# Moving the PEER gate product to ScalarE and writing a sigmoid gate as a tanh

## The chip, the cores and the metric

The kernel runs on one core of one Trainium2 chip, in one launch. A core has TensorE (PE in the profile, with its weight loads as PEld), VectorE (DVE), ScalarE (ACT), GpSimd (POOL), SyncE (SP) and 16 DMA engines that move data between HBM and the on-chip memories. The metric is the device time of one execution in microseconds, as a median over runs. All arithmetic is float32 in and out.

## The reference, cut to what matters

The network is a first block (three attention branches, then a PEER feed-forward layer) and a second block of two layers (an mLSTM and a retention mixer, each followed by an expert-choice mixture of experts, for a context and a latent sequence). Everything has 256 tokens of width 1024. Two places matter here. In the PEER layer every token picks 128 of 16384 experts (8 heads, 16 each). An expert is one row of `u` and one row of `v`:

```
act = gelu(einsum('chkd,cd->chk', u[ic], hc), approximate=False)
w   = gc * act                                 # gc: softmax of the picked scores
out = einsum('chk,chkd->cd', w, v[ic])
```

In the mLSTM mixer the output of every head (128 wide) is divided by its root mean square and multiplied by a sigmoid gate `o`, a projection of the input:

```
y = y * rsqrt(mean(y*y, axis=-1) + EPS)        # per token and head, EPS = 1e-6
y = y * norm_g * sigmoid(o)
```

## The kernel before, in words

The kernel is written in a tile framework. A program's Python generators issue instructions, and the framework simulates each engine's time line to order them; every engine then runs its own list strictly in that order, waiting on semaphores where an operand is not there. So a change of one instruction's engine can reorder others.

**Picks.** The function `picks` works through two blocks of 128 tokens and, in each, 128 picks: pick k is the k-th expert of each of the 128 tokens, one token per partition. A pick is this chain:

1. POOL issues an indirect DMA (L1359) that gathers one row of 2048 numbers per partition, `u` and `v` side by side, 1 MB in all, into one of RING = 8 buffers.
2. DVE multiplies the `u` half by the token's input and sums it into one number per partition (the `stt` at L1360; by the helper's line, 128x1024 at L614 in the profile).
3. ACT takes the gelu of that 128x1 column (L1363; L598 in the profile).
4. DVE multiplies the column by the pick's gate (`tt`, L1364; L605 in the profile, 128x1).
5. ACT scales the 128x128 identity by the column (L1368), which gives a diagonal matrix. There are four such buffers.
6. PE multiplies the diagonal with the `v` half, two matmuls of 128x512 (L1370; L617 in the profile), and adds them up in PSUM over the 128 picks.

When step 6 has read the buffer, POOL may issue a gather into it. The first gather of a pick is thus released eight picks earlier by PE.

Beside the picks runs other work through `drive(..., [side], PACE)`: the routing of the heads (queries, top-16 searches on DVE, `prepare`, `prepare_last`, `route`), and the whole context side of the second block's first layer (`context_task`: an mLSTM with its projections, gates, convolution, attention by heads, the norm below, output projection and the opening of its mixture of experts). These use the same DVE, ACT, POOL and PE, and stand between the picks' instructions in each engine's list.

**Output gates.** `mlstm_norm` runs twice: for the context beside the picks, and for the latent sequence in the stage after them, beside `mlstm_attend`. Each run goes over two slabs of four heads, and each slab over two tiles of 128 tokens, so there are eight tiles of 128x512 in all. For every tile the projection stands in PSUM; ACT takes exp(-o), DVE adds one (L1890, by the helper L609) and takes a reciprocal (L1891). `norm_pair` then makes the root of the mean square for two heads and multiplies head, root and gate. The function is called for the retention layer too, with another gate.

In the profile, an operation that goes through a helper has the helper's line: `act` L598, `tt` L605, `ts` L609 and L611, `stt` L614, `mm` L617. ACT needs a function's table loaded before it can run it; a load (ACT_TABLE_LOAD) stands in ACT's list wherever the next function is not in the set that is there.

Of the kernel before, what the change touches and what calls it, by code (L numbers as in the profile page):

```python
# [14 lines left out]
AF = mybir.ActivationFunctionType  # L15
OP = mybir.AluOpType
AX = mybir.AxisListType

EPS = 1e-6
# [3 lines left out]
RING, BATCH = 8, 1  # L23
# [490 lines left out]
class K:  # L514
# [817 lines left out]
    def picks(self, h2, prep):  # L1332


        ident = self.c("ident")
        ring = dg = None
        for i, r in enumerate(self.routes):
            while r["heads"] < 1:
                yield next(prep) * 0
            if ring is None:  # L1340
                ring, dg = deque(self.f(2048, True) for _ in range(RING)), deque(self.f(128, True) for _ in range(4))
            if i:
                self.nc.sync.dma_start(h2[0].a, self.keep[2])
            po = self.ps(2)
            rows, gate, act = (r[n].a for n in ("rows", "gate", "act"))
            for k in range(0, 128, BATCH):
                while r["heads"] * 16 < k + 1:
                    yield next(prep) * 0
                if i and k == 128 - BATCH:

                    ring.popleft().free()
                    self.x = [self.f(1024) for _ in range(2)]
                    self.nc.sync.dma_start(self.x[0].a, self.keep[0])
                got = []
                for j in range(k, k + BATCH):
                    b = ring[0].a
                    ring.rotate(-1)
                    got.append(b)
                    self.nc.gpsimd.indirect_dma_start(b, None, self.t["puv"], bass.IndirectOffsetOnAxis(ap=rows.bitcast(U32)[:, j:j + 1], axis=0))  # L1359
                    self.stt(b[:, :1024], b[:, :1024], 1.0, h2[0].a, OP.mult, OP.mult, accum_out=act[:, j:j + 1])  # L1360
                    yield 2600
                o = act[:, k:k + BATCH]
                self.act(o, o, AF.Gelu)  # L1363
                self.tt(o, o, gate[:, k:k + BATCH], OP.mult)  # L1364
                for j, b in enumerate(got):
                    d = dg[0].a
                    dg.rotate(-1)
                    self.act(d, ident, AF.Copy, scale=act[:, k + j:k + j + 1])  # L1368
                    for f in range(2):
                        self.mm(po.a[:, f * 512:(f + 1) * 512], d, b[:, 1024 + f * 512:1024 + (f + 1) * 512], k + j == 0, k + j == 127)  # L1370
            if i == 0:
                x = ring[0].a[:, :1024]
                ring.rotate(-1)
            else:
                x = self.x[1].a
            self.nc.sync.dma_start(x, self.keep[i])
            for f in range(2):
                o = x[:, f * 512:(f + 1) * 512]
                self.tt(o, po.a[:, f * 512:(f + 1) * 512], o, OP.add)
            if i == 0:  # L1380
                self.nc.sync.dma_start(self.keep[0], x)
            po.free()
            for n in ("rows", "gate", "act"):
                r[n].free()
        h2[0].free()
        for b in (*ring, *dg):
            b.free()
# [492 lines left out]
    def mlstm_norm(self, S):  # L1880

        S["yT"] = self.r(2048), self.r(2048)
        for s in range(2):

            b = self.f(1024)
            for i, p in enumerate(self.wide([S["hT"]], self.halves("w2", 8 + 2 * s, S["seg"]))[0]):
                o = b.a[:, i * 512:(i + 1) * 512]
                self.act(o, p.a, AF.Exp, scale=-1.0)
                p.free()
                self.ts(o, o, 1.0, OP.add)  # L1890
                self.nc.vector.reciprocal(o, o)  # L1891
            if s == 1:
                for x in S["hT"]:
                    x.free()
            yield 9800
            for j in (4 * s, 4 * s + 2):
                while S.get("heads", 0) < j + 2:
                    yield 5200
                self.norm_pair(S["y"], b, 512, j % 4 * 128, S["ss"].a[:, :16].rearrange("p (i h) -> p i h", i=2)[:, :, j:j + 2], j)
                self.pair_T(S["yT"], [S["y"].a[:, i * 1024:(i + 1) * 1024] for i in range(2)], j, self.col("mlstm_g"))  # L1900
                yield 3000
            b.free()
        for b in (S["ss"], S["y"]):
            b.free()

    def norm_pair(self, y, gate, w, o, ss, j):

        t = self.f(16)
        v4 = t.v("p (k i h) -> p k i h", k=4, i=2)
        self.ts(v4[:, 0], ss, 1.0 / 128, OP.mult, EPS, OP.add)  # L1910
        out = t.a[:, 8:12]
        self.root(out, t.a[:, 4:8], t.a[:, :4])
        for i in range(2):
            for h in range(2):
                k = slice(i * 1024 + (j + h) * 128, i * 1024 + (j + h + 1) * 128)
                self.stt(y.a[:, k], y.a[:, k], out[:, 2 * i + h:2 * i + h + 1], gate.a[:, i * w + o + h * 128:i * w + o + h * 128 + 128], OP.mult, OP.mult)
        t.free()
# [553 lines left out]
```

## Time and profile before

| | us |
|---|---|
| median of 3 runs | 2615.86 (2615.13 to 2617.09) |
| profiled execution, its own time | 2619.42 |
| its span, first to last instruction | 2617.7 |
| PE busy | 2265.2 |
| DVE busy | 1243.2 |
| ACT busy | 802.9 |
| POOL busy | 634.4 |
| DMA, mean rate over the span | 328 GB/s |

The picks stage lies at about 411 to 1208 us of the span, the latent mLSTM stage at about 1208 to 1400, and the latent and retention layers behind it. Busy shares are averages over stages with different limits, so the stages have to be read by themselves. In a table of windows the granted clock (PEclk) is TensorE's clock as a share of 2.4 GHz (1.00 is 2.4, 0.50 is 1.2 GHz).

### The profile page before, as it was taken

The numbers are of one execution on the slowest core, as the hardware profiler recorded it, in microseconds if no ns is written. First come the engines' busy times: TensorE is split into PE (matmuls) and PEld (weight loads), VectorE is DVE, ScalarE is ACT, GpSimd is POOL, SyncE is SP. The second block draws the span as 40 slices with busy tenths as digits, with TensorE's granted clock in tenths as the row PEclk, the third lists the DMA queues.
The fourth block names the chain that finished last, engine by engine and source line by source line (L and its number), as shares of the span: only waits on it lengthen the run. The fifth ranks groups of instructions, "written<-read, shape, count | busy, mean of one in ns | idle before, by whom it ended". The sixth has DMA issues, their size and how long they took to land. (4 is left out here: it accounts for less than half of the span.)

```text
span 2617.7 us, 29085 instructions
## 1 busy us (share of the span) xinstructions
PE 2265.2 (87%) x10507; PEld 1276.5 (49%) x10507; DVE 1243.2 (47%) x2943; ACT 802.9 (31%) x1632; POOL 634.4 (24%) x526
## 2 busy tenths in 40 slices
PE   7999987799787789777878999999969989878877
PEld 5867776356332445224666344444459863222223
DVE  4365448899955676555866122212186461000001
ACT  5564443344622763223643000000042441000000
POOL 3223444344343444332530000000032420000000
PEclk9999988999999899999998999999989999999999
DMA  7467758898999789996446899999966398999997
GB/s 295 177 240 258 262 185 324 329 364 333 332 410 419 288 338 394 421 421 251 143 163 266 354 396 420 414 421 421 373 235 240 105 378 334 420 419 420 419 420 319
DMA packets 129534, 858.81 MB, mean 328 GB/s; under 512 B 15342, under 2 KB 15934, under 8 KB 33520
## 3 DMA queue, kind: packets, MB, share of 16 engines
q1 hardware_dynamic: 87120, 573.50, 55.2%
q0 software_dynamic: 42272, 283.47, 27.8%
q8 instruction: 83, 1.36, 0.2%
q14 instruction: 59, 0.48, 0.0%
HBM read 853.63 MB, written 3.28 MB: 327 GB/s over the span
## 5 line engine op out<-in xcount | busy, mean ns | idle before, releaser
L617 PE MATMUL pp<-fa 128*128 128x512 f32 (+10 forms) x4912 | 1289.2, 492 | 220.8 <-ACT fa L598 153.0
L617 PEld LDWEIGHTS pp<-fa 128*128 128x128 f32 (+3 forms) x4912 | 554.0, 159 | 836.5 <-issue 395.3
L617 PE MATMUL pp<-rw,rt 128*128 128x512 f32 (+1 forms) x1896 | 469.6, 401 | 17.4 <-ACT rw L598 5.6
L614 DVE SCALAR_TENSOR_TENSOR fa<-fa 128x1024 f32<-128x1024 f32 (+5 forms) x561 | 406.4, 747 | 109.0 <-DMA fa<-in_puv,fa 104.6
L605 POOL TENSOR_TENSOR rw<-fa,rw 128x1024 fp32r<-128x1024 f32 x84 | 211.5, 2519 | 809.4 <-ACT rw L598 772.0
L617 PEld LDWEIGHTS pp<-rw,rt 128*128 128x128 f32 x1896 | 351.1, 190 | 114.5 <-issue 15.3
L1359 POOL DMA_INDIRECT fa<-in_puv,fa x256 | 278.4, 1087 | 412.5 <-PE pp L617 330.3
L605 DVE TENSOR_TENSOR fa<-pp,fa 128x512 f32<-128x512 f32 (+3 forms) x225 | 128.4, 578 | 525.8 <-PE pp L617 505.2
L598 ACT ACTIVATE fa<-fa 128x1 f32<-128x1 f32 (+9 forms) x601 | 214.1, 375 | 480.7 <-DVE fa L614 351.6
L598 ACT ACTIVATE fa<-pp 128x512 f32<-128x512 f32 (+4 forms) x169 | 93.4, 565 | 710.9 <-PE pp L617 581.3
L598 ACT ACTIVATE rw<-fa 128x1024 fp32r<-128x1024 f32 x208 | 216.4, 1054 | 243.4 <-PE pp L617 164.3
L617 PE MATMUL pp<-rt,fa 128*64 128x512 f32 (+3 forms) x736 | 241.7, 579 | 16.8 <-DMA rt<-in_moe_up 9.7
L605 DVE TENSOR_TENSOR rw<-fa,rw 128x1024 fp32r<-128x1024 f32 x124 | 166.8, 1350 | 171.1 <-ACT rw L598 170.8
L617 PE MATMUL pp<-rt,rw 128*128 128x256 f32 x1632 | 232.2, 301 | 13.8 <-POOL rw L605 4.0
L617 PEld LDWEIGHTS pp<-rt,rw 128*128 128x128 f32 x1632 | 212.6, 200 | 32.7 <-issue 12.1
L617 PE MATMUL pp<-rw,fa 128*64 128x512 f32 (+2 forms) x720 | 207.5, 582 | 13.5 <-DMA rw<-in_moe_down 5.3
L605 DVE TENSOR_TENSOR fa<-fa 128x1 f32<-128x1 f32 (+10 forms) x453 | 124.0, 284 | 81.3 <-ACT fa L598 74.7
L611 DVE TENSOR_SCALAR fa<-pp,fa 128x128 f32<-128x128 f32 (+1 forms) x80 | 36.5, 463 | 247.0 <-PE pp L617 164.1
L598 ACT ACTIVATE fa<-ct,fa 128x128 f32<-128x128 f32 x256 | 101.7, 399 | 103.6 <-DVE fa L605 64.0
L627 PE MATMUL pp<-ct,fa 128*128 128x128 f32 (+2 forms) x441 | 75.6, 308 | 59.7 <-ACT fa L598 27.1
L617 PEld LDWEIGHTS pp<-rt,fa 128*64 128x64 f32 (+1 forms) x736 | 66.1, 125 | 120.7 <-issue 79.3
L617 PEld LDWEIGHTS pp<-rw,fa 128*64 128x64 f32 (+1 forms) x720 | 58.9, 123 | 125.1 <-issue 83.9
(135 smaller groups left out, 961.2 us busy)
## 6 DMA issues: line engine op xcount, KB each, us to landing
fa<-in_w SPq DMA_DIRECT2D x98, 1024.0 KB, 5.3
fa<-in_moe_gate SPq DMA_DIRECT2D x62, 1024.0 KB, 14.1
fa<-in_moe_down SPq DMA_DIRECT2D x59, 1024.0 KB, 16.8
fa<-in_moe_up SPq DMA_DIRECT2D x56, 1024.0 KB, 17.1
fa<-in_ada_w SPq DMA_DIRECT2D x43, 1024.0 KB, 5.0
rw<-in_moe_up SPq DMA_DIRECT2D x36, 1024.0 KB, 16.2
rt<-in_moe_down SPq DMA_DIRECT2D x31, 1024.0 KB, 15.2
rt<-in_moe_up SPq DMA_DIRECT2D x28, 1024.0 KB, 16.2
```

The source lines that it names most:

```text
L598: return self.nc.scalar.activation(out, in_, func, **kw)
L605: (eng or self.nc.vector).tensor_tensor(out, a, b, op=op)
L611: (eng or self.nc.vector).tensor_scalar(out, a, s1, s2, op0=op0, op1=op1, **kw)
L614: self.nc.vector.scalar_tensor_tensor(out, a, s, b, op0=op0, op1=op1, **kw)
L617: self.nc.tensor.matmul(ps, l, r, start=start, stop=stop, skip_group_check=True)
L627: self.nc.tensor.transpose(ps, x, self.c("ident")[:k, :k])
L1359: self.nc.gpsimd.indirect_dma_start(b, None, self.t["puv"], bass.IndirectOffsetOnAxis(ap=rows.bitcast(U32)[:, j:j + 1], axis=0))
```

## The change

Two edits. In the picks, step 4 leaves DVE: ACT multiplies the column by the gate itself, as a Copy with the gate column as its scale, right behind the gelu (256 instructions move from DVE to ACT). In `mlstm_norm`, sigmoid(o) is written as half of (1 + tanh(o/2)). ACT makes tanh(o/2) from PSUM and then adds one in an Identity; DVE's add and reciprocal go (eight of each), and the half goes into the head norm's root, which is taken of 4(mean + EPS) by the same instruction with other constants. The retention layer keeps the factor 1.

```
-                o = act[:, k:k + BATCH]
-                self.act(o, o, AF.Gelu)
-                self.tt(o, o, gate[:, k:k + BATCH], OP.mult)
+                for j in range(k, k + BATCH):
+                    o = act[:, j:j + 1]
+                    self.act(o, o, AF.Gelu)
+                    self.act(o, o, AF.Copy, scale=gate[:, j:j + 1])
...
-                self.act(o, p.a, AF.Exp, scale=-1.0)
+                self.act(o, p.a, AF.Tanh, scale=0.5)
                 p.free()
-                self.ts(o, o, 1.0, OP.add)
-                self.nc.vector.reciprocal(o, o)
+                self.act(o, o, AF.Identity, bias=1.0)
...
-                self.norm_pair(S["y"], b, 512, ..., j)
+                self.norm_pair(S["y"], b, 512, ..., j, 4.0)
...
-    def norm_pair(self, y, gate, w, o, ss, j):
+    def norm_pair(self, y, gate, w, o, ss, j, by=1.0):
...
-        self.ts(v4[:, 0], ss, 1.0 / 128, OP.mult, EPS, OP.add)
+        self.ts(v4[:, 0], ss, by / 128, OP.mult, by * EPS, OP.add)
```

ScalarE's list at the start of the second token block's picks, before: `fa 128x1` is a gelu, `ct,fa 128x128` a diagonal, `fa 128x128` an exponential of the context mLSTM's attention.

```order
L598 ACT_TABLE_LOAD
L598 ACTIVATE fa<-fa 128x1 x4
L598 ACT_TABLE_LOAD
L598 ACTIVATE fa<-fa 128x128 x2
L598 ACT_TABLE_LOAD
L598 ACTIVATE fa<-fa 128x1
L598 ACT_TABLE_LOAD
L598 ACTIVATE fa<-fa 128x128 x4
L598 ACT_TABLE_LOAD
L598 ACTIVATE fa<-fa 128x1
L598 ACTIVATE fa<-ct,fa 128x128 x2
L598 ACTIVATE fa<-fa 128x1
```

The same place of ScalarE's list with the change, where `fa 128x1 x2` is a gelu and the copy that applies its gate.

```order
L598 ACT_TABLE_LOAD
L598 ACTIVATE fa<-fa 128x1 x2
L598 ACTIVATE fa<-ct,fa 128x128
L598 ACTIVATE fa<-fa 128x1 x2
L598 ACTIVATE fa<-ct,fa 128x128
L598 ACTIVATE fa<-fa 128x1 x2
L598 ACTIVATE fa<-ct,fa 128x128
L598 ACTIVATE fa<-fa 128x1 x2
L598 ACT_TABLE_LOAD
L598 ACTIVATE fa<-fa 128x128 x2
L598 ACTIVATE fa<-ct,fa 128x128
L598 ACT_TABLE_LOAD
```

The first diagonal stood behind six gelus and five table loads; it now stands right behind the first gelu and copy. Over the whole program the table loads on ScalarE go from 88 to 79, all nine of them in the picks stage.

VectorE's list in the latent mLSTM stage, at the second slab's gates, before: `rt_4634` belongs to the query and key convolution, `rw_70` is a rounding remainder of the weights, and `fa<-pp,fa 128x512` is the attention's product.

```order
L614 SCALAR_TENSOR_TENSOR fa<-fa 128x128 x4
L614 SCALAR_TENSOR_TENSOR rt_4634<-pp,ct,rt_4633 128x256
L605 TENSOR_TENSOR rw_70<-fa,rw_70 128x1024
L609 TENSOR_SCALAR fa<-fa 128x512 x2
L1891 RECIPROCAL fa<-fa 128x512 x2
L614 SCALAR_TENSOR_TENSOR fa<-pp,fa 128x512 x2
L614 SCALAR_TENSOR_TENSOR rt_4634<-pp,ct,rt_4633 128x256
L614 SCALAR_TENSOR_TENSOR fa<-pp,fa 128x4
```

The same place of VectorE's list with the change.

```order
L614 SCALAR_TENSOR_TENSOR fa<-fa 128x128 x4
L605 TENSOR_TENSOR rw_70<-fa,rw_70 128x1024
L614 SCALAR_TENSOR_TENSOR fa<-pp,fa 128x512 x2
L614 SCALAR_TENSOR_TENSOR rt_4634<-pp,ct,rt_4633 128x256
L614 SCALAR_TENSOR_TENSOR fa<-pp,fa 128x4
L605 TENSOR_TENSOR fa<-pp,fa 128x4
```

Two adds and two reciprocals no longer stand ahead of the attention's products. From the mixture of experts of the latent layer on, every engine's list is the same but for buffer numbers.

## Rows read from the trace of the kernel before

**Rows 1.** Windows by stage: from:to us, length, busy us per engine, clock, DMA share, GB/s.

```profile
411.00:743.00 332.00, 279.42 (x1034) 164.38 (x1035) 292.35 (x938) 140.92 (x306) 142.08 (x120) 0.93 0.91 349
743.00:848.00 105.00, 78.94 (x176) 29.77 (x174) 57.92 (x143) 26.28 (x87) 36.73 (x39) 0.98 1.01 421
848.00:1032.00 184.00, 151.36 (x522) 86.90 (x522) 126.64 (x321) 108.79 (x243) 76.70 (x70) 0.93 0.88 334
...
1208.00:1400.00 192.00, 151.57 (x821) 125.57 (x822) 139.58 (x317) 98.56 (x205) 63.73 (x52) 0.92 0.46 159
```

**Rows 2.** Windows of line L1359 alone: the gathers issued in two of these stretches.

```profile
411.00:743.00 332.00, 118.97 (x99) 0.93 0.91 349
...
848.00:1032.00 184.00, 56.28 (x49) 0.93 0.88 334
```

**Rows 3.** Timeline, picks alone: start, us, engine, line, operation, count, [idle before <- releaser].

```profile
802.32 0.20 ACT L598 ACTIVATE fa<-fa 128x1 f32<-128x1 f32 x1 [1.59 <-DVE fa L614]
802.81 0.40 ACT L598 ACTIVATE fa<-ct,fa 128x128 f32<-128x128 f32 x1 [0.29 <-PE pp L617]
804.81 0.20 ACT L598 ACTIVATE fa<-fa 128x1 f32<-128x1 f32 x1 [1.59 <-DVE fa L614]
```

**Rows 4.** Groups on VectorE, 411 to 743: count, busy us, mean ns, idle before.

```profile
L614 DVE SCALAR_TENSOR_TENSOR fa<-fa 128x1024 f32<-128x1024 f32 x93 | 114.0, 1226 | 7.8 <-DMA fa<-in_puv,fa 7.8
...
L605 DVE TENSOR_TENSOR fa<-fa 128x1 f32<-128x1 f32 x92 | 19.0, 209 | 10.9 <-ACT fa L598 10.6 <-issue 0.3
...
L1891 DVE RECIPROCAL fa<-fa 128x512 f32<-128x512 f32 x2 | 6.7, 3346 | 0.0
```

**Rows 5.** Windows of 5 us at the start of the second token block.

```profile
850.00:855.00 5.00, 0.00 (x0) 0.00 (x0) 4.46 (x9) 2.37 (x5) 1.36 (x1) 0.50 0.84 326
855.00:860.00 5.00, 0.00 (x0) 0.00 (x0) 5.00 (x9) 3.73 (x7) 2.48 (x3) 0.50 0.04 18
860.00:865.00 5.00, 0.64 (x1) 0.50 (x2) 2.20 (x12) 4.96 (x12) 0.93 (x2) 0.50 0.44 52
865.00:870.00 5.00, 5.00 (x13) 2.31 (x12) 1.74 (x3) 1.16 (x4) 1.59 (x3) 0.75 0.08 13
```

**Rows 6.** Timeline of ScalarE there.

```profile
852.24 0.20 ACT L598 ACTIVATE fa<-fa 128x1 f32<-128x1 f32 x1 [0.39 <-DVE fa L614]
...
858.42 1.28 ACT L598 ACT_TABLE_LOAD   x1
859.72 0.20 ACT L598 ACTIVATE fa<-fa 128x1 f32<-128x1 f32 x1
...
863.93 0.68 ACT L598 ACTIVATE fa<-ct,fa 128x128 f32<-128x128 f32 x2
```

**Rows 7.** Timeline of VectorE there.

```profile
858.89 0.22 DVE L605 TENSOR_TENSOR fa<-fa 128x1 f32<-128x1 f32 x2
859.03 1.21 DVE L614 SCALAR_TENSOR_TENSOR fa<-fa 128x1024 f32<-128x1024 f32 x1
```

**Rows 8.** Timeline of GpSimd there: the last gather issued and the next.

```profile
846.52 0.99 POOL L1359 DMA_INDIRECT fa<-in_puv,fa  x1 [1.58 <-DVE fa L605]
...
868.18 1.01 POOL L1359 DMA_INDIRECT fa<-in_puv,fa  x1 [2.70 <-PE pp L617]
```

**Rows 9.** Groups on ScalarE, 848 to 1032.

```profile
L598 ACT ACT_TABLE_LOAD x32 | 41.1, 1283 | 1.3 <-DMA fa<-arow 0.8
```

**Rows 10.** Timeline of the latent mLSTM stage, VectorE.

```profile
1318.08 3.35 DVE L1891 RECIPROCAL fa<-fa 128x512 f32<-128x512 f32 x1
...
1366.27 6.55 DVE L1891 RECIPROCAL fa<-fa 128x512 f32<-128x512 f32 x2
1372.75 1.22 DVE L614 SCALAR_TENSOR_TENSOR fa<-pp,fa 128x512 f32<-128x512 f32 x2
```

**Rows 11.** Timeline of the latent mLSTM stage, TensorE.

```profile
1326.44 4.52 PE L617 MATMUL pp<-fa 128*128 128x256 f32 x32 [1.87 <-DVE fa L614]
...
1373.51 14.26 PE L617 MATMUL pp<-fa 128*128 128x129 f32 x92 [10.54 <-DVE fa L614]
```

**Rows 12.** Groups on ScalarE, 1210 to 1400: activations from SBUF of the gates' size.

```profile
L598 ACT ACTIVATE fa<-fa 128x512 f32<-128x512 f32 x2 | 1.3, 626 | 0.0
```

More of the change, by code (lines that the diff above doesn't have):

```diff
@@ L1898, in mlstm_norm @@
                     yield 5200
-                self.norm_pair(S["y"], b, 512, j % 4 * 128, S["ss"].a[:, :16].rearrange("p (i h) -> p i h", i=2)[:, :, j:j + 2], j)
+                self.norm_pair(S["y"], b, 512, j % 4 * 128, S["ss"].a[:, :16].rearrange("p (i h) -> p i h", i=2)[:, :, j:j + 2], j, 4.0)
                 self.pair_T(S["yT"], [S["y"].a[:, i * 1024:(i + 1) * 1024] for i in range(2)], j, self.col("mlstm_g"))
```

## The prediction, made before the change was run

> **What bounds the kernel now.** I read the windows by stage first, because the change touches two stages only. The reader is to see that the picks stage has four stretches. In 743 to 848 the DMA share is full, 421 GB/s, and every engine has slack: VectorE is busy 57.92 of 105 us, ScalarE 26.28 [rows 1]. The stretch 1032 to 1208 looks the same, so one row stands for both. There a pick takes what its gather takes: one gelu starts 2.49 us after the other (802.32, 804.81) [rows 3]. In 411 to 743 and 848 to 1032, where routing and the context's mLSTM run beside the picks, the DMA share is 0.91 and 0.88, with 99 and 49 gathers issued [rows 1, 2]. That leaves 0.09 x 332 = 30 us and 0.12 x 184 = 22 us in which the DMA engines stood idle: these 52 us are the most that the picks can give back, since the bytes stay the same. In the first VectorE is busy 292 of 332 us, so it is the engine that delays picks; in the second VectorE has 127 and ScalarE 109 of 184, and the idle time must come from order and not from load. The latent mLSTM stage (1208 to 1400) has a DMA share of 0.46: it is bound by its chain of compute. After it every list is unchanged, so what is saved before should arrive at the end whole.
>
> Then I looked into each place: groups on VectorE in the first stretch [rows 4], 5 us windows and timelines where the second has its hole [rows 5 to 8], and the timeline around the reciprocals behind it [rows 10, 11].
>
> **Part 1, first mixed stretch.** The 92 products of 128x1 are 19.0 us busy, and VectorE idled 10.9 us in front of them, nearly all for ScalarE's gelu [rows 4]. They overlap with what follows: a pair of them starts at 858.89 and the next product at 859.03, 0.07 us of a slot each [rows 7]. So VectorE gets back between 92 x 0.07 = 6.4 and 19.0 us of busy time, and up to 10.9 of waiting. The context's gates of the first slab lie here too: two reciprocals, 6.7 us [rows 4], and two adds of some 0.4 us, which I estimate from the attention products of 128x512 (1.22 for two [rows 10], 0.6 each), so 0.8 to 1.2. Taking the low end of the slots, 6.4 + 10.9 + 6.7 + 0.8 = 25 us come free on an engine with 40 us of slack. In the new order this stretch ends four picks later (86 picks instead of 82 have had their dot product), which puts 4 x 1.2 us more of dot products [rows 4] into it: about 20 us net. Not every microsecond of VectorE is a microsecond of DMA; some picks wait for PE or for POOL. The bounds are 0 (the freed time falls where gathers were under way) and 30 (all the idle DMA share). I take 15, three quarters of the net relief, because VectorE is 88% busy here.
>
> **Part 2, second mixed stretch.** At its start the gathers stop for 21.7 us: one is issued at 846.52, the next at 868.18, released by PE [rows 8]. In 855 to 860 and 865 to 870 the DMA engines are nearly empty (0.04, 0.08), in 860 to 865 the share is 0.44, in 850 to 855 it is 0.84; that makes 5 x (0.16 + 0.96 + 0.56 + 0.92) = 13 us of idle DMA [rows 5]. The reason stands in the lists. The gelu of the first pick starts at 852.24, but its gate product waits on VectorE behind dot products until 858.89, and its diagonal waits on ScalarE behind table loads until 863.93 [rows 6, 7]: 11.7 us from gelu to diagonal, against 0.49 in the undisturbed rhythm (802.32 to 802.81) [rows 3]. With the change the first diagonal stands behind one gelu and one copy, and PE can free the first buffer about 0.5 + 1.0 us after the gelu starts. I expect the next gather near 855, 13 us earlier, and four more follow at the pace of the dot products, 1.2 us each. But buffers freed at the front of a block run dry again further on: I count 10 of the stretch's 22 us. Bounds: 0, where the following table loads only push the hole back, and 22.
>
> ScalarE pays for its new work out of the table loads that go. A copy takes a slot of 0.11 to 0.40 us: 0.11 is the distance at which short activations follow each other here, the 0.20 of a gelu is the nearest row, 0.40 that of the diagonal, which has the same kind of scale [rows 3]. In this stretch 49 x 0.20 = 9.8 us come, in both mixed ones 148 x 0.20 = 30. The nine loads that go each cost 1.30 us from the start of the load to the start of the next activation (858.42 to 859.72) [rows 6], 11.7 in all. ScalarE is busy 141 of 332 and 109 of 184 us, 41.1 of the latter in 32 loads [rows 1, 9], so it has room; on the path of one pick the copy takes the place of a semaphore there and back to VectorE (0.49 from gelu to diagonal) and costs the same within 0.1.
>
> The Trainium skill, "ScalarE: Activation LUTs", section "What ACT_TABLE_LOAD costs", gives a switch of sets 1283 ns for the load and 1380 ns of drain, 2.66 us in all. The 1283 ns are in the trace [rows 9], the drain is not: the next activation starts 1.30 us after the load does. By the page the nine loads would be worth 24 us on ScalarE rather than 11.7; I go by the rows.
>
> **Part 3, the latent gates.** The first pair of reciprocals, from 1318.08, ends on VectorE just ahead of the attention's products, and PE waits 1.87 us for them [rows 10, 11]. The whole wait goes: 1.9. Before the second pair PE waits 10.54 us until 1373.51 [rows 11], and VectorE spends 6.55 of those on reciprocals, after two adds. With the change the products stand behind the remainder of the weights alone. The wait does not vanish, since ScalarE has to do two tanhs and two Identities of 0.63 us [rows 12] between exponentials that the attention needs, and PE's operands were late for other reasons too: I leave it 3 us, and gain 7.5. Together 9.4; bounds 0, where ScalarE becomes late instead, and 12.4, both waits. The eight Identities cost ScalarE 8 x 0.63 = 5 us, hidden where ScalarE waits: here it is busy 99 of 192 us [rows 1]. The context's second slab lies in Part 2's stretch or the picks beyond it, where VectorE has room, and I price it at nothing.
>
> **Sum.** 15 + 10 + 9.4 = 34.4 us off the profiled execution's 2619.4: 2585.0. The median of the runs lies 3.6 us below the profiled execution (2615.86 against 2619.42), so the forecast is 2581 us.
>
> **Rivals.**
>
> - *A, only the latent gates count.* The mixed stretches may be bound by the DMA queue: shares of 0.91 and 0.88 are near full, and the 12% in which TensorE or POOL delayed a gather can remain. For it: the gathers' share is set by POOL as well, busy 142 of 332 us in the first stretch [rows 1]. Against it: the hole of rows 5, which the lists explain. Then 9.4 + some 1: 2619.4 - 10 - 3.6 = 2606 us.
> - *B, the full relief.* All but a few microseconds of idle DMA come back (28 and 18 us) and the latent stage gains 12 plus the following waits, 15: 61 in all, 2555 us. For it: the waits of VectorE for ScalarE vanish as well as their instructions. Against it: the granted clock is 0.50 in the hole [rows 5] and PE then takes longer for the first picks.
> - *C, ScalarE becomes the bound, and the kernel is slower.* In the mixed stretches ScalarE has exponentials and table loads in its list; each of the 148 picks there gets a 0.20 us copy on the same engine. If ScalarE's list were the path, they would cost 148 x 0.20 = 30 us and the Identities 5, against 11.7 from the loads and 10 from the latent stage: +13, 2629 us. It decides from the point where ScalarE is busy throughout between gathers; in 860 to 865 it is, 4.96 of 5 us [rows 5]. Against it: 41.1 of its 109 us there are loads that come of the order itself. The Trainium skill, "ScalarE: Activation LUTs", section "Rules for kernel authors", speaks for this rival: it wants products and additions on VectorE and not on ScalarE. The rows show a column of 128x1 at 0.20 us on either engine, so the rule has no ground in speed here.
> - *D, a new hole.* The framework's new order may open a hole elsewhere, such as another run of dot products with no diagonals between, and give back the gain: 2611 to 2621.
>
> **How the numbers follow.** The forecast has 0.59, with a range of its own from 2566 to 2595 (its three terms between a third below and half above). A has 0.18, B 0.10, C 0.06, D 0.07. The range of 8 in 10 leaves out C, D, and the tails of A and B: 2555 to 2609. A measurement of this kernel can tell 0.2%, 5.2 us, from no change. Faster than 2610.6: forecast, A and B but for their edge, 0.86. Within: D and that edge, 0.08. Slower than 2621.1: 0.06.
>
> **What would show it.** In the changed kernel's windows, the stretch up to the full rate should be about 15 us shorter for equally many gathers, with a DMA share above 0.94; the pause of the gathers at the start of the second block should fall from 21.7 to about 9 us; the wait of TensorE behind the second pair of gates should be near 3 us; from there on every event should be earlier by the same amount. Table loads should stay at 1.28 us. The prediction is wrong if ScalarE's busy share nears full in a mixed stretch, if the DMA share there stays below 0.9, or if the part behind 1400 us changes in length by more than 3 us.

## The result, and the profile after

The changed kernel took 2583.55 us (median of 4 runs, 2580.81 to 2587.40) against 2615.49 for the kernel before; the ratio is 0.9878, 95% interval 0.9861 to 0.9895. On another chip the same pair gave 0.9893 (0.9872 to 0.9913). The profiled execution took 2583.78 us, with a span of 2582.0 against 2617.7. The forecast was 2581 us.

The sum came out; its terms did not all. Four cuts of the span show it. The picks' gathers all have one line, and the last small reciprocals of the attention (128x4) mark the end of the latent mLSTM's heads. First the kernel before (instruction, count, duration min/median/max in ns, first and last start; then the first gather of the second token block on the time line):

```profile
L1359 POOL DMA_INDIRECT fa<-in_puv,fa x256: 932/937/4516, 411.2 to 1206.4; - x128
...
820.46 0.94 POOL L1359 DMA_INDIRECT fa<-in_puv,fa  x1 [4.05 <-PE pp L617]
...
L1860 DVE RECIPROCAL fa<-fa x16: 165/178/182, 840.6 to 1389.1; 128x4 f32<-128x4 f32 x16
```

Then the changed kernel, where the reciprocal's line is 1861:

```profile
L1359 POOL DMA_INDIRECT fa<-in_puv,fa x256: 935/939/3614, 409.5 to 1179.4; - x128
...
809.83 0.94 POOL L1359 DMA_INDIRECT fa<-in_puv,fa  x1 [4.04 <-PE pp L617]
...
L1861 DVE RECIPROCAL fa<-fa x16: 166/178/178, 830.0 to 1353.9; 128x4 f32<-128x4 f32 x16
```

The reader subtracts neighbours in each fence: gathers of block 1 (409.3 us before, 400.3 after), of block 2 (386.0, 369.6), latent heads (182.7, 174.5), and what is left of the span (1228.6, 1228.1). So block 1 gave 9.0 us, block 2 16.4, the latent heads 8.2, and the rest of the program stayed as long as it was and simply came earlier. Another execution of the same kernel gave 12.8, 16.6 and 7.5: block 1 is known to some 4 us, the others to 1. The kernel before has this one profile only, and that execution took 2619.42 us, 3.9 us above its median; a gain taken against it may hold some of that, a comparison among the changed kernels does not.

The windows that answer to [rows 1], cut where the same gathers are issued (99 and 49 in the first and third):

```profile
409.00:733.00 324.00, 276.40 (x1032) 162.72 (x1033) 276.69 (x843) 164.93 (x397) 149.47 (x120) 0.94 0.92 358
733.00:837.00 104.00, 78.45 (x179) 29.14 (x180) 52.87 (x107) 36.88 (x123) 37.00 (x40) 0.99 1.01 421
837.00:1006.00 169.00, 152.11 (x523) 88.09 (x522) 115.05 (x265) 116.23 (x292) 76.62 (x70) 0.94 0.93 368
...
1181.00:1354.00 173.00, 143.26 (x782) 122.13 (x783) 115.90 (x282) 98.69 (x207) 61.34 (x51) 0.89 0.44 152
```

The mixed stretches are 8 and 15 us shorter, the one at full rate is what it was. In the third, VectorE fell from 127 to 115 us and ScalarE rose from 109 to 116 in a shorter stretch: ScalarE is now busy 69% of it, against 59% before. It matters below.

At the start of the second block, ScalarE and GpSimd of the changed kernel, to be read against [rows 6] and [rows 8]:

```profile
840.75 0.53 ACT L598 ACTIVATE fa<-fa 128x1 f32<-128x1 f32 x2 [0.39 <-DVE fa L614]
841.31 0.40 ACT L598 ACTIVATE fa<-ct,fa 128x128 f32<-128x128 f32 x1
```

```profile
835.57 0.99 POOL L1359 DMA_INDIRECT fa<-in_puv,fa  x1 [2.92 <-DVE fa L605]
843.16 3.23 POOL L605 TENSOR_TENSOR fa<-fa,ct 128x256 f32<-128x256 f32 x2 [6.61 <-DMA fa<-arow]
846.55 1.78 POOL L1359 DMA_INDIRECT fa<-in_puv,fa  x1 [0.16 <-issue]
```

From the first gelu to its diagonal it is 0.56 us now, not 11.7. TensorE, which frees the buffers, waited for that diagonal; its first matmuls of the block, before and after:

```profile
864.36 6.13 PE L617 MATMUL pp<-fa 128*128 128x512 f32 x13 [15.35 <-ACT fa L598]
```

```profile
841.76 8.54 PE L617 MATMUL pp<-fa 128*128 128x512 f32 x15 [4.25 <-ACT fa L598]
```

The gathers pause for 11.0 us instead of 21.7. They would start earlier still, but GpSimd is in the middle of two products of the context's, and the gather follows them within 0.16 us of issue.

TensorE in the latent stage: the group of the attention's matmuls, before (1206 to 1389) and after (1179 to 1354); the columns are count, busy us, mean ns, and the idle time ahead of them by what ended it:

```profile
L617 PE MATMUL pp<-fa 128*128 128x129 f32 (+2 forms) x317 | 60.9, 349 | 24.3 <-DVE fa L614 17.8 <-ACT fa L598 6.3 <-DVE rt L614 0.2
```

```profile
L617 PE MATMUL pp<-fa 128*128 128x129 f32 (+2 forms) x317 | 60.9, 351 | 16.2 <-ACT fa L598 8.4 <-DVE fa L614 7.8
```

Waits for VectorE fell by 10.0 us, waits for ScalarE rose by 2.1. The difference, 7.9 us, is close to the stage's gain of 8.2.

### The profile page after: what moved, and what is told of

Read it like the earlier page. It is cut to its first block, busy times and chain, and to the rows that moved or that the text cites. A ratio compares the mean times of both kernels' runs of the same rounds, so it can differ in the third digit from the quotient of the medians.

```text
span 2582.0 us, 29060 instructions
## 1 busy us (share of the span) xinstructions
PE 2258.1 (87%) x10507; PEld 1274.8 (49%) x10507; DVE 1182.7 (46%) x2671; ACT 869.9 (34%) x1887; POOL 643.3 (25%) x526
## 5 line engine op out<-in xcount | busy, mean ns | idle before, releaser
L614 DVE SCALAR_TENSOR_TENSOR fa<-fa 128x1024 f32<-128x1024 f32 (+4 forms) x561 | 407.5, 752 | 157.7 <-DMA fa<-in_puv,fa 153.0
L598 ACT ACTIVATE fa<-fa 128x1 f32<-128x1 f32 (+8 forms) x865 | 292.1, 353 | 476.3 <-DVE fa L614 336.9
L1359 POOL DMA_INDIRECT fa<-in_puv,fa x256 | 288.8, 1128 | 408.0 <-PE pp L617 321.8
L598 ACT ACTIVATE rw<-fa 128x1024 fp32r<-128x1024 f32 x208 | 216.7, 1054 | 243.4 <-PE pp L617 173.1
L598 ACT ACT_TABLE_LOAD x79 | 101.4, 1283 | 14.0 <-DVE fa L609 4.9
## 6 DMA issues: line engine op xcount, KB each, us to landing
fa<-in_moe_gate SPq DMA_DIRECT2D x62, 1024.0 KB, 12.8
```

What stands on the lines that cost most here:

```text
L598: return self.nc.scalar.activation(out, in_, func, **kw)
L614: self.nc.vector.scalar_tensor_tensor(out, a, s, b, op0=op0, op1=op1, **kw)
```

## The experiments

All ratios are against the kernel before on the same chip. The stage times are from each run's profile, cut as above; that of the kernel before is from the first chip. The last column counts ScalarE's table loads between the first and the last gather of block 2.

| run | median us | ratio (95%) | block 1 | block 2 | latent heads | loads, block 2 |
|---|---|---|---|---|---|---|
| before | 2609 to 2615 | 1 | 409.3 | 386.0 | 182.7 | 33 |
| changed, again | 2582.90 | 0.9893 (0.9872 to 0.9913) | 396.4 | 369.3 | 175.2 | 27 |
| gates_only | 2596.07 | 0.9946 (0.9929 to 0.9962) | 401.9 | 375.8 | 177.8 | 31 |
| tanh_only | 2601.13 | 0.9958 (0.9944 to 0.9972) | 403.5 | 383.6 | 174.2 | 35 |
| tanh_latent | 2592.14 | 0.9923 (0.9906 to 0.9941) | 402.0 | 375.5 | 173.0 | 31 |
| slab0_old | 2583.36 | 0.9897 (0.9880 to 0.9913) | 399.3 | 371.0 | 171.7 | 27 |
| extra_copy | 2600.36 | 0.9957 (0.9940 to 0.9974) | 400.4 | 384.1 | 173.1 | 29 |
| no_gate | 2575.60 | 0.9863 (0.9841 to 0.9884) | 398.7 | 365.2 | 173.6 | 27 |
| dve_diag | 2593.08 | 0.9929 (0.9912 to 0.9945) | 403.5 | 374.7 | 176.2 | 31 |
| identity_dve | 2584.30 | 0.9896 (0.9875 to 0.9916) | 397.8 | 374.5 | 175.8 | 27 |
| gate_pool | 2773.29 | 1.0629 (1.0604 to 1.0655) | 488.0 | 471.9 | | 29 |
| pace_020 | 2579.72 | 0.9881 (0.9864 to 0.9897) | 396.9 | 369.7 | 174.1 | 27 |

The changed kernel itself stands at 400.3, 369.6 and 174.5, also with 27 loads. Two cautions. The kernel before takes 2609 to 2612 us on the other chips, so gains by stage against its one profile add up to more than the ratio: for the changed kernel run again, 37 us by stage and 28 by the ratio. And what is left of the span behind the latent heads is not the same in every profile: 1228.1 and 1228.3 in the changed kernel, but 1221.7 in identity_dve, 1222.8 in tanh_only and 1224.8 in no_gate. No run says why.

The changed kernel, run again as a measure for no_gate, gate_pool and identity_dve, was expected so:

> The changed kernel as it is, once more, as the measure for the other three on the same chip: 0.986 to 0.990 of the kernel before.

**Either part alone.** `gates_only` is the first hunk of the diff, `tanh_only` the others.

> The picks' gate product on ScalarE, the output gates as before (exp, add, reciprocal). Theory: the gate product waiting on VectorE behind dot products is what delays picks, so this part alone brings nearly all of the 27 us that the changed kernel gains by its last gather (of those some 16 at the second block's mixed stretch): about 2592 us, between 2588 and 2597, and the pause of the gathers at the second block's start falls from 21.7 to about 11 us as in the changed kernel. Rival 'reciprocals': the context's reciprocals on VectorE were what filled it in the first stretch, so that this part brings the second stretch alone, about 2600. Rival 'table loads': the gain is that of the table loads which go; of those only three go here (85 instead of 88), 4 us, so about 2611. From the latent stage on nothing is gained: the wait of TensorE behind the second pair of gates stays near 10.5 us.

> The output gates by tanh, the picks' gate product on VectorE as before. Theory: the latent stage gains about 8 us as in the changed kernel, the picks at most 3 (two reciprocals and two adds less on VectorE): about 2606 us, between 2602 and 2609, with the pause of about 21 us at the second block's start still there. Rival 'reciprocals': 8 + 9 to 11 us, about 2597. Rival 'table loads': with 90 loads instead of 88 the picks lose 3 us, about 2610.

The gates alone took 10.2 us off block 2 and 7.4 off block 1, and the pause at the second block's start was 10.8 us; tanh alone took 8.4 off the latent heads, 5.8 off block 1 and 2.3 off block 2, with a pause of 20.7. The expected medians go by the first chip's 2615.5, and here the kernel before takes 2612.0, so the ratios are the fair measure: the gates alone gave 14 us where 23.5 were expected, which misses; tanh alone gave 11 where 9.5 were, which holds, though its one profile, of an execution 4.7 us below its median, has 8.1 beside the picks where at most 3 were expected. The hole is the gates' alone: the ninth gather of block 2 starts 47.7 us after the first in the kernel before, 46.7 with tanh alone, 36.4 with the gates alone and 36.7 in the changed kernel. One more expectation failed: the gates alone took 4.9 us off the latent heads too, whose gates they leave as they were, and TensorE's wait behind the second pair was 8.15 us there. As the only cause, 'table loads' falls, since neither run follows its count for the whole program (85 and 90 against 88). 'Reciprocals' is half right. In block 2 the parts add up to 12.5 us, the whole gives 16.4.

**The context's gates by slab.** `tanh_latent` keeps exp, add and reciprocal for the context; `slab0_old` for its first slab alone:

```
-                self.act(o, p.a, AF.Tanh, scale=0.5)
+                if S["seg"] and s == 0:          # tanh_latent: if S["seg"]:
+                    self.act(o, p.a, AF.Exp, scale=-1.0)
...
+                    self.ts(o, o, 1.0, OP.add)
+                    self.nc.vector.reciprocal(o, o)
+                else:
```

> As the changed kernel, but the context's output gates go back to exp, add and reciprocal; only the latent ones use tanh. Theory: the context's gates stand beside the picks where VectorE has room once the gate products are gone: within 4 us of the changed kernel, 2584 to 2588. Rival 'reciprocals': the first stretch loses its gain of about 10 us: 2594. Rival 'table loads': 85 loads instead of 79, 8 us: 2592.

> As the changed kernel, with the context's first slab of output gates (beside the first mixed stretch) by exp, add and reciprocal and its second slab by tanh. With both context slabs old, the changed kernel lost 7 us of the second block's 16.4 and 2 to 5 of the first block's 9. Theory 'two reciprocals on VectorE just where picks' dot products wait': this run keeps the second block's gain (14 us or more off its 386) and loses 2 to 5 us in the first. Rival 'the order of all': the second block loses 4 us or more though its own reciprocals are gone.

With both slabs old, block 2 takes 375.5 us, as with the gates alone, and by the ratios the kernel is 8 to 12 us above the changed one; the theory's 4 us do not hold. The ratio's interval fits both rivals, 'table loads' (2592) and 'reciprocals' (2594); but the latter put a loss of 10 us in the first stretch, and block 1 lost 2 to 6. With only the first slab old, block 2 takes 371.0 and the median is the changed kernel's. So the second slab's tanh is worth some 4 to 6 us in block 2, and the first slab's nothing clear of block 1's scatter. What in the second slab is worth it is not shown, because two things go together there. One is the reciprocals. In the kernel before, that slab stands in the second mixed stretch; VectorE's time line there:

```profile
927.46 3.35 DVE L1891 RECIPROCAL fa<-fa 128x512 f32<-128x512 f32 x1
930.73 1.16 DVE L614 SCALAR_TENSOR_TENSOR fa<-fa 128x1024 f32<-128x1024 f32 x1
...
933.28 1.22 DVE L614 SCALAR_TENSOR_TENSOR fa<-fa 128x1024 f32<-128x1024 f32 x1
...
934.50 3.35 DVE L1891 RECIPROCAL fa<-fa 128x512 f32<-128x512 f32 x1
...
937.78 0.15 DVE L605 TENSOR_TENSOR fa<-fa 128x1 f32<-128x1 f32 x1
```

The reader sees a dot product right behind the first reciprocal and a pick's gate product right behind the second, in a stretch where VectorE is idle a third of the time on average.

The other is ScalarE's table loads: 31 in block 2 with this slab old (gates_only, tanh_latent), 27 with it new; four at 1.30 us make 5.2 us. ScalarE at the slab's first tile in tanh_latent, where it takes an exponential:

```profile
887.29 1.28 ACT L598 ACT_TABLE_LOAD   x1
888.59 0.60 ACT L598 ACTIVATE fa<-pp 128x512 f32<-128x512 f32 x1
889.20 1.28 ACT L598 ACT_TABLE_LOAD   x1
```

And in the changed kernel, where it takes a tanh:

```profile
883.58 0.46 ACT L598 ACTIVATE rt<-pp,ct 128x256 fp32r<-128x256 f32 x1
883.93 0.59 ACT L598 ACTIVATE fa<-pp 128x512 f32<-128x512 f32 x1
884.55 0.72 ACT L598 ACTIVATE fa<-fa 128x512 f32<-128x512 f32 x2
```

The exponential stands between two loads; the tanh stands between other activations, without one. No run takes away the reciprocals and leaves these loads.

**Is ScalarE near its bound?** `extra_copy` repeats the gate's copy, `no_gate` leaves it out:

```
                     self.act(o, o, AF.Gelu)
                     self.act(o, o, AF.Copy, scale=gate[:, j:j + 1])   # no_gate: left out
+                    self.act(o, o, AF.Copy, scale=gate[:, j:j + 1])   # extra_copy
```

> As the changed kernel, with the copy that applies the gate done twice for each pick (the gate is then squared, which is all that differs in the output): 256 more activations of 128x1 on ScalarE, in the chain of every pick. Theory: ScalarE has room, so a copy of some 0.3 us costs only where a pick's chain ends last: at full DMA rate nothing, in the mixed stretches a few us: 2586 to 2592. Rival 'ScalarE is the bound in the mixed stretches': 148 x 0.28 us = 41 us more, 2625.

> As the changed kernel without the gate product (the picks are added up ungated, which is all that differs in the output): 256 copies less on ScalarE and none on VectorE. Theory 'ScalarE is near its bound in the second mixed stretch': a second copy cost 17 us there by the last gather, 49 x 0.3 = 15 by duration, so taking the first one away gives back 5 to 10 us against the changed kernel, all of it between 836 and 1010 us. Rival 'the second copy only opened another hole in the order': within 3 us of the changed kernel. At the full DMA rate neither expects anything.

The second copy cost 17 to 21 us over the changed kernel (ratio 0.9957 against 0.9893 and 0.9878), more than the 8 that the theory allowed and far less than the rival's 41. It cost nothing at full rate and nothing clear in block 1; 14.5 of it stand in block 2, as much as 49 copies of 0.3 us, though two more table loads are in it. Taking the first copy away gave 7.3 us against the changed kernel beside it, 4.1 of them in block 2 and 3.5 behind the latent heads, where the edit has no place. ScalarE's busy time in 850 to 930 fits: extra_copy, the changed kernel, no_gate.

```profile
850.00:930.00 80.00, 65.22 (x221) 37.83 (x220) 51.06 (x134) 71.25 (x175) 37.27 (x36) 0.96 0.95 349
```

```profile
850.00:930.00 80.00, 70.05 (x237) 41.66 (x236) 55.71 (x142) 64.84 (x161) 40.63 (x39) 0.94 0.98 388
```

```profile
850.00:930.00 80.00, 72.94 (x249) 42.00 (x248) 58.07 (x145) 61.56 (x138) 41.26 (x40) 0.98 1.00 387
```

ScalarE is busy 89% with two copies and the DMA share is 0.95; without a copy it is 77% and the DMA engines are full. The changed kernel lies between (81%, 0.98). A caution: extra_copy and no_gate both have 82 table loads where the changed kernel has 79, three loads or some 4 us, so the size of either effect is rough, and that the second copy also opened a hole of its own in the order is not ruled out.

**Where else the product can stand.** `dve_diag` gives VectorE the diagonal with both factors and relieves ScalarE of two activations in three; `gate_pool` gives the product to GpSimd.

```
-                    self.act(o, o, AF.Copy, scale=gate[:, j:j + 1])
...
-                    self.act(d, ident, AF.Copy, scale=act[:, k + j:k + j + 1])
+                    self.ts(d, ident, act[:, k + j:k + j + 1], OP.mult, gate[:, k + j:k + j + 1], OP.mult)
```

> As the changed kernel, but VectorE makes the diagonal, identity times the activation times the gate in one instruction of 128x128; of the three activations of a pick only the gelu stays on ScalarE, and VectorE is again between gelu and diagonal. Theory 'the wait in VectorE's list is what cost': ScalarE is relieved by some 0.6 us a pick and it doesn't help; the pause at the second block's start is back (over 15 us between gathers) and the picks lose at least 15 us against the changed kernel: 0.995 to 1.01 of the kernel before. Rival 'ScalarE's load is what costs': 49 x 0.6 = 29 us less work on it in the second stretch, so faster than the changed kernel, 0.984 or lower.

The pause is back (18.5 us) and ScalarE's relief doesn't make up for it: block 1 loses 3 to 7 and block 2 5 us against the changed kernel, and by the ratios the kernel is 9 to 13 us slower than it. The loss is less than the 15 us that I set; the rival's gain isn't there. ScalarE, VectorE and GpSimd at the second block's start:

```profile
847.26 0.20 ACT L598 ACTIVATE fa<-fa 128x1 f32<-128x1 f32 x1 [0.39 <-DVE fa L614]
```

```profile
852.25 1.73 DVE L614 SCALAR_TENSOR_TENSOR fa<-fa 128x1024 f32<-128x1024 f32 x1
...
853.91 0.59 DVE L611 TENSOR_SCALAR fa<-ct,fa 128x128 f32<-128x128 f32 x2
```

```profile
841.78 0.97 POOL L1359 DMA_INDIRECT fa<-in_puv,fa  x1 [2.67 <-DVE fa L614]
...
860.29 1.00 POOL L1359 DMA_INDIRECT fa<-in_puv,fa  x1 [0.15 <-PE pp L617]
```

The first diagonal comes at 853.91, behind five dot products of later picks, though its gelu started at 847.26. This is the hole of the kernel before, made again with another instruction.

```
-                    self.act(o, o, AF.Copy, scale=gate[:, j:j + 1])
+                self.tt(o, o, gate[:, k:k + BATCH], OP.mult, self.nc.gpsimd)
```

> As the changed kernel, with the gate product on GpSimd instead of ScalarE. Theory 'off VectorE': what counts is that the product doesn't stand behind dot products; GpSimd has room, but a column of 128x1 costs it more than 0.2 us and a semaphore each way, so 0 to 10 us more than the changed kernel, still 15 us or more below the kernel before, and no pause of over 15 us at the second block's start. Rival 'right behind the gelu': the gain needs the product on ScalarE itself; GpSimd's product waits behind gathers that wait for a buffer, so the picks lose their gain, within 8 us of the kernel before.

Both theories expected far too little: 190 us more than the changed kernel. Its picks alone (743 to 848) no longer run at the full rate. What the waits say of 760 to 840 there, by engine: who waited for whom, us, times, longest; ScalarE first, then GpSimd, then PE.

```profile
ACT fa L598 <- POOL fa L605: 65.0, 22, 6.7
```

```profile
POOL fa L1359 <- PE pp L617: 40.3, 22, 3.4
POOL fa L605 <- ACT fa L598: 6.1, 10, 0.6
```

```profile
PE pp L617 <- ACT fa L598: 27.8, 13, 4.1
```

ScalarE's diagonal waits for GpSimd's product; the product stands behind a gather that waits for PE to free a buffer; and PE waits for the diagonal. A ring of waits through one in-order list takes the run-ahead out of the gathers, 301 GB/s instead of 421 in that stretch:

```profile
743.00:848.00 105.00, 68.44 (x113) 26.09 (x112) 44.29 (x68) 16.39 (x58) 47.13 (x57) 0.83 0.81 301
```

**The one, and the order.** `identity_dve` adds the one on VectorE (`self.ts(o, o, 1.0, OP.add)` for the Identity); `pace_020` sets PACE to 0.20.

> As the changed kernel, with the one added by VectorE (0.42 us of 128x512 each) instead of ScalarE's Identity (0.63). Theory: it is the reciprocal of 3.35 us that counted and not where the one is added: within 3 us of the changed kernel. Rival 'ScalarE is near its bound': the four Identities beside the picks and the four in the latent stage cost up to 5 us, which come back.

> The changed kernel with the side work beside the picks spread by 0.20 instead of 0.21; as many table loads (79) in a slightly other order. Not a test of a cause: it shows how far the order alone moves the time, within 6 us of the changed kernel, 0.986 to 0.991 of the kernel before.

Both medians are within 4 us of the changed kernel's, as expected: the place of the addition does not show in the time. But identity_dve's one profile, of an execution 2.0 us above its median, divides it otherwise: 374.5 us in block 2, 5 more than the changed kernel, and 6.6 less behind the latent heads. With neither reciprocals nor more table loads, block 2 is there as long as in tanh_latent, so the order of the lists alone can move it by as much as the second slab's gates seem worth. Of the kernels with the whole computation pace_020 has the lowest median, 2579.72, but its interval covers both of the changed kernel's ratios, so it can't be called a better version.

## Why the prediction was right, by its own steps

- **What bounds the stages.** Right. The full-rate stretches gave nothing, the mixed ones and the latent stage gave all, and the rest moved earlier unchanged (1228.6, 1228.1).
- **Part 1, 15 us.** Measured 9.0, and 12.8 in the other execution: within its bounds, too high. Gates and tanh alone gave 7.4 and 5.8 there, so both of the freed terms (products with their waits, and reciprocals) may count; with some 4 us between two executions the runs do not price them apart.
- **Part 2, 10 us.** Measured 16.4 and 16.6; this is the term that was mis-sized. The hole was read well: the diagonal is right behind its gelu, the pause fell by 10.7 us to 11.0, and gates_only, which has this part without the tanh, gained 10.2 in the block. I had the next gather 13 us earlier; GpSimd's product for the context held it, and I had not followed GpSimd's list. The step that failed is the sentence that priced the context's second slab at nothing because VectorE had room: tanh_latent, with that slab old, is 5.9 us longer in block 2 than the changed kernel, and 4.5 longer than slab0_old. Idle time on average says neither whether a dot product stands behind a 3.35 us instruction nor what ScalarE does for the same gate. Which of the two it was, the reciprocals or the four table loads, or only the order, stays open.
- **ScalarE has room.** Half right. At one copy a pick it may be near the edge: one more cost 14.5 us in block 2, with two more table loads, and one less gave back 4.1. The step from gelu to diagonal cost 0.56 us, against 0.49 before, as forecast within 0.1.
- **Table loads.** Nine fewer, 1283 ns each as before. I used them only to pay for the copies, and over the whole program their number does not order the runs. But six of the nine go in block 2, and there the runs with 27 loads take 369.3 to 371.0 us and those with 31 take 374.7 to 375.8; identity_dve (27, 374.5) and no_gate (27, 365.2), which has no copies, are the exceptions. The Trainium skill, "ScalarE: Activation LUTs", section "What ACT_TABLE_LOAD costs", adds a drain of 1380 ns to each; no trace here shows it, the step from the start of a load to the next activation being 1.30 us [rows 6].
- **Part 3, 9.4 us.** Measured 8.2 and 7.5, and 8.4 with tanh alone; since the gates alone took 4.9 off the same stage, not all of it is shown to be these gates'. The 10.54 us wait behind the second pair fell to 0.25, not 3. But the next wait took part of it back: for the row that a DMA brings into ScalarE's exponentials. TensorE's time line in the changed kernel, then VectorE's and ScalarE's:

```profile
1333.72 4.26 PE L617 MATMUL pp<-fa 128*128 128x256 f32 x32 [0.25 <-DVE fa L614]
1345.54 5.10 PE L617 MATMUL pp<-fa 128*128 128x129 f32 x22 [7.56 <-DVE fa L614]
```

```profile
1344.80 0.69 DVE L614 SCALAR_TENSOR_TENSOR fa<-pp,fa 128x512 f32<-128x512 f32 x1 [4.50 <-ACT fa L598]
```

```profile
1343.86 3.46 ACT L598 ACTIVATE fa<-fa 128x256 f32<-128x256 f32 x10 [5.14 <-DMA fa<-arow]
```

  The engine named at 1345.54 is VectorE, but VectorE's instruction waited for these exponentials, and they for the DMA.
- **Rivals.** A is out (the picks gave 25 us). B had too much. C named a real mechanism in a real place, but the point from which it decides lies further on: extra_copy, with one copy more, lost 14.5 us in block 2. The rule beside it, by which products belong on VectorE (the Trainium skill, "ScalarE: Activation LUTs", section "Rules for kernel authors"), is a rule of speed per element; for this column its place in the lists counted more: with the product on ScalarE gates_only came to 0.9946. D did not come.
- **What would show it.** The first mixed stretch is 8 us shorter, not 15, and its DMA share is 0.92, where I wanted above 0.94; the pause is 11.0 us, where I said about 9. Of the signs of being wrong none came: ScalarE is busy 69% in the second mixed stretch, the DMA share stays above 0.9, and the part behind the latent heads changed by 0.5 us. The forecast's own range, a third below to half above its 34.4 us, should read 2564 to 2593 and not 2566 to 2595; nothing hangs on it.

So the median was met within 3 us because Part 1 was some 2 to 6 us too high and Part 2 6 us too low; that the two errors cancelled was luck. What stays open is how the reciprocals, the table loads and the changed order as such share in block 2 beyond the hole: gates and tanh alone give 12.5 us there and the whole 16.4, and each variant has its own order.

## What to carry to other kernels

A tiny instruction is priced by the list it stands in, not by its duration: 0.2 us on VectorE cost 11 us where dot products stood ahead of it, and the same product on GpSimd made a ring of waits that cost 190 us. Move a chain's small steps onto the engine that does the steps beside them. And where a long instruction is placed among a chain's steps, look at its own window and at the other engines' instructions that go with it, not at the stretch's mean idle time.

## What the runs showed that I had not expected

A reciprocal of 128x512 takes 3.35 us on VectorE, over five times a product of that size; a tanh from PSUM and an Identity take 0.6 us each on ScalarE. An engine that is busy 81% may already be near its edge: some 15 us more of copies on ScalarE cost 14.5 us in block 2 and 15 us less gave 4.1, with the loads and the order changed a little in both.
